# Sums of squares of X's third chunk added by TensorE, and the scores of two query blocks in one visit to the 64x32 tiling

## The chip, the core and the metric

One NeuronCore of a Trainium2 chip runs the whole program; there is one launch. The time of a run is the device time of that core in microseconds (us), and smaller is better. TensorE (PE; its weight loads are the row PEld) multiplies matrices into PSUM. VectorE (DVE), ScalarE (ACT) and GpSimd (POOL) work element by element. SyncE (SP) issues the DMA transfers.

## What is computed

A two-layer decoder trunk runs for 1024 prompt tokens and 32 sample tokens (8 sequences of 4), 1056 columns of width 1024. Both layers begin with an RMSNorm. Layer 0 projects to a causal convolution branch and to a dilated sliding-window attention with 16 heads of 64; layer 1 is a gated linear recurrence. The change touches the first norm and the attention scores of the prompt:

```python
def rms_norm(x, g):
    y = xf * lax.rsqrt(jnp.mean(xf * xf, axis=-1, keepdims=True) + NORM_EPS)

def dswa_prompt(q, k, v, window, dilation):      # (128,1), (512,4), (2048,16), merged
    scores = jnp.einsum('ndbqhe,ndbkhe->ndbhqk', qb, kk) * (hd ** -0.5)
    scores = jnp.where(mask, scores, -jnp.inf)
    p = jnp.exp(scores - lse[..., None])
```

## The kernel before

**Layout.** Everything is held with features on the 128 partitions and tokens along the free dimension. The tokens are cut into three chunks of 384, 384 and 288 columns (`CW`). A dense projection of 128 output features is 24 products for each chunk: eight slices of the contraction, each split into a high and a low part of the reduced float32 format, three products a slice. The projections of layer 0 run pair of heads by pair of heads in the order ag, av (convolution branch), v, k, q.

**The first norm.** x isn't normalised before the projection; the factor `R` (one over the root mean square of a token) is multiplied in where a result leaves PSUM. `prologue()` loads x as twelve tiles `X[c, k]`, chunk c, k from 0 to 3; each holds two feature slices side by side, so 768 or 576 columns. ACT squares each tile. DVE adds them: tile 0 takes tile 1, tile 2 takes tile 3, tile 0 takes tile 2 (`add`), and then tile 0's two halves are added (`fold`). `stat(c)` sums over the partitions on TensorE with a full float32 product against a constant matrix (`self.ones`); such a product shows in the trace as two passes, written x<-b,c. ACT then makes `R` of it by a logarithm and an exponential (`rstd_of`), and POOL multiplies the rotary tables by it (`turn`).

**The attention.** `attention(pr)` handles a pair of heads in 8 blocks of 128 queries. `qk(i)` makes the scores of block i: for each of four groups of 32 queries and two heads a product with a 64-row contraction and 32 output rows, so TensorE works in its 64x32 tiling with eight tiles. The near keys are the 128 (block 0) or 256 keys that end with the block, read one after the other. For blocks from 2 on a second set follows in the same visit, the far keys, 32*i of them and read with a step of 4. Each product has two passes, so a set is 16 passes. The two heads' scores go to two PSUM banks (kind x, four in all). DVE then adds the mask and takes the row minimum (one custom instruction per head), and ACT takes the exponential. `tr(i)` transposes the probabilities, `far(i)` those of the far keys, `pv(i)` multiplies by the values into the bank o, and `far_pv` adds the far part.

**Who sets the order.** The order on every engine is fixed when the program is built. `dense()` emits the projections; after every slice `sides()` puts in atoms, the small pieces of the threads (statistics, attention, convolution, recurrence), by a planner that keeps a clock for each engine (`self.clk`) from prices written in `array()` and `cost()`. A TensorE atom goes in when its due time is at least 300 ns behind TensorE's clock, a bank of kind x is free within 60 ns, and neither ACT's nor DVE's planned clock is over 1500 ns ahead:

```python
if a.kind == "pe":
    ok = r <= now + LEAD and self.xrel[0] <= now + 60 and max(c["act"], c["dve"]) <= now + 1500
```

The price of an addition on DVE is `n / 0.96 + 150` ns for n columns. A result of the first projection (ag, pair 0) leaves PSUM, in the planner's order, after the statistics of all three chunks. Every instruction is issued through the helper at line 158, so that the profile shows L158 throughout; tiles are told apart by their letters (d, x, o are PSUM banks, b and c buffers in SBUF).

Of the kernel before, what the change touches and what calls it, by code (L numbers as in the profile page):

```python
# [11 lines left out]
AF = mybir.ActivationFunctionType  # L12
OP = mybir.AluOpType
# [16 lines left out]
NMASK = 7 * 32 + 256  # L30
# [147 lines left out]
class Kern:  # L178
# [306 lines left out]
    def plan(self, jobs):  # L485
        for j in jobs:
            if j.w is None:
                j.w = W = {"raw": None, "hl": None, "src": j.src}
                self.wq.append(W)

    def w_load(self, W):
        if W["raw"] is None and W["hl"] is None:
            self.own(self.wown, lambda: W.update(raw=self.A.alloc(1024)))
            self.begin(self.clk["pe"])
            self.nc.sync.dma_start(W["raw"].f, W["src"])
            W["t"] = self.cur
# [163 lines left out]
    def prologue(self):  # L660
        nc, A, io = self.nc, self.A, self.io
# [4 lines left out]
        X = {}  # L666
# [7 lines left out]
        def do(f, key, *deps):  # L674
            self.begin(max(at[d] for d in deps))
            f()
            at[key] = self.finish()
# [25 lines left out]
        def square(c, k, act):  # L703
            x = X[c, k]
            if act:
                f = lambda: nc.scalar.activation(x.f, x.f, AF.Square)
            else:
                f = lambda: nc.gpsimd.tensor_tensor(x.f, x.f, x.f, op=OP.mult)
            do(f, ("s", c, k), ("l", c, k))

        def add(c, k, m, eng):
            x, y = X[c, k], X[c, m]
            do(lambda: eng.tensor_tensor(x.f, x.f, y.f, op=OP.add), ("s", c, k), ("s", c, k), ("s", c, m))
            y.free()

        def fold(c):
            w = CW[c]
            x = X[c, 0]
            do(lambda: nc.vector.tensor_tensor(x[:, :w], x[:, :w], x[:, w:2 * w], op=OP.add), ("s", c, 0), ("s", c, 0))

        def stat(c):
            def f():
                w = CW[c]
                x = X[c, 0]
                p = self.px()
                nc.tensor.matmul(p[:, :w], self.ones.f, x[:, :w], start=True, stop=True)
                self.rstd_of(self.R[:, C0[c]:C0[c] + w], p[:, :w])
                x.free()
            return f

        def turn(c):
            def f():
                cs = slice(C0[c], C0[c] + CW[c])
                for t in (self.cos, self.sin):
                    nc.gpsimd.tensor_tensor(t[:, cs], t[:, cs], self.R[:, cs], op=OP.mult)
            return f

        n = KT // 2
        at = {}
# [33 lines left out]
        V = nc.vector  # L773
        for c in range(3):
            for k in range(n):
                square(c, k, True)
            add(c, 0, 1, V)
            add(c, 2, 3, V)
            add(c, 0, 2, V)
            fold(c)  # L780
        for c in range(3):
            self.fin["pro", c] = at["s", c, 0]
            self.spawn(f"pro{c}", 0.1 * c, [Atom(stat(c), "pe", [("pro", c)], ("r0", c)),
                                            Atom(turn(c), "pool", None, ("cs", c))])

# [169 lines left out]
    def attention(self, pr):  # L955
        nc, A = self.nc, self.A
        S = self.pair[pr]
        P, O, B, F = {}, {}, {}, {}

        def width(i):  # L960
            return 32 * i * (i > 1), 128 * min(i + 1, 2)

        def qk(i):
            def f():
                if i == 0:
                    S["den"] = A.alloc(16)
                    S["o"] = A.alloc(T)
                nf, nn = width(i)
                W = nf + nn
                kc = slice(128 * (i + 1) - nn, 128 * (i + 1))  # L970
                hs = [slice(64 * h, 64 * h + 64) for h in range(2)]
                ss = []
                for h in range(2):
                    P[i, h] = A.alloc(W + 8)
                    ss.append(self.px())
                q, k = S["q"], S["k"]
                for a, b, ks in ((nf, W, kc), (0, nf, None)):
                    for r in range(4):
                        for h in range(2):
                            if b > a:  # L980
                                nc.tensor.matmul(ss[h][32 * r:32 * r + 32, a:b],
                                                 q[hs[h], 128 * i + 32 * r:128 * i + 32 * r + 32],
                                                 k[hs[h], ks or slice(r, 128 * i, 4)], start=True, stop=True,
                                                 skip_group_check=True, tile_position=(64 * h, 32 * r))
                t = self.cur
                for h in range(2):
                    e = P[i, h]
                    m = e[:, W:W + 1]
                    self.resume(t)
                    nc.vector.tensor_tensor_reduce(e[:, :W], ss[h][:, :W], self.mask[:, NMASK - W:NMASK],  # L990
                                                   op0=OP.add, op1=OP.min, scale=-0.125, scalar=1e30, accum_out=m)
                    nc.scalar.activation(e[:, :W], e[:, :W], AF.Exp, scale=-1.0, bias=m,
                                         accum_out=S["den"][:, h * 8 + i:h * 8 + i + 1])
            return f

        def tr(i):
            def f():
                nf, nn = width(i)
                p = self.px()
                m = nn // 128  # L1000
                for j in range(m):
                    for h in range(2):
                        n = 2 * j + h
                        nc.tensor.transpose(p[:, 128 * n:128 * n + 128], P[i, h][:, nf + 128 * j:nf + 128 * j + 128],
                                            self.ident)
                B[i] = A.alloc(512)
                self.copy(B[i][:, :256 * m], p[:, :256 * m])
                if not nf:
                    for h in range(2):
                        P[i, h].free()  # L1010
            return f

        def far(i):
            def f():
                p = self.px()
                parts = [n for n, (t0, t1, g, m) in enumerate(FAR) if t0 <= i < t1]
                for n, x in enumerate(parts):
                    g, m = FAR[x][2:]
                    for h in range(2):
                        a = 256 * n + 128 * h  # L1020
                        nc.tensor.transpose(p[:, a:a + 128], P[i, h][:, 128 * g:128 * g + 128], self.ident)
                for h in range(2):
                    P[i, h].free()
                t = self.cur
                for n, x in enumerate(parts):
                    t0, t1, g, m = FAR[x]
                    if i == t0:
                        F[x] = A.alloc(256 * (t1 - t0))
                    self.resume(t, "pe")
                    self.copy(F[x][0:m, :].rearrange("p (h t c) -> p h t c", h=2, c=128)[:, :, i - t0, :],  # L1030
                              p[0:m, 256 * n:256 * n + 256].rearrange("p (h c) -> p h c", h=2))
            return f
# [41 lines left out]
        atoms = [Atom(store, "sp", [("rk", pr, c) for c in range(3)] + [("rq", pr, c) for c in range(3)], ("ko", pr))]  # L1074
        K = lambda n, i: (n, pr, i)
        for i in range(9):
            if i < 8:
                atoms.append(Atom(qk(i), "pe", [K("pv", i - 2)] if i > 1 else [("ko", pr)], K("qk", i),
                                  (2, 7) if i == 0 else None))
            if i:  # L1080
                t = i - 1
                atoms.append(Atom(tr(t), "pe", [K("qk", t)], K("tr", t)))
                if t > 1:
                    atoms.append(Atom(far(t), "pe", [K("qk", t)], K("far", t)))
                atoms.append(Atom(pv(t), "pe", [K("tr", t), ("vt", pr)] + [K("fp", 0)] * (t == 4), K("pv", t)))
                if t % 4 == 3:
                    atoms.append(Atom(far_pv(t // 4), "pe", [K("pv", t)] + [K("far", x) for x in range(max(2, t - 3), t + 1)],
                                      K("fp", t // 4)))
# [1547 lines left out]
```

## Time and profile before

| | before |
|---|---|
| median of 3 runs | 2325.9 us (2324.64 to 2326.06) |
| the profiled execution | 2328.87 us, its span 2327.0 us |
| TensorE busy | 2262.7 us (97%), 17415 passes |
| VectorE busy | 1601.6 us (69%) |
| ScalarE busy | 1026.3 us (44%) |
| GpSimd busy | 1026.5 us (44%) |
| mean granted TensorE clock | 0.994 |

The profile is of one execution, 3.0 us above the median. A matmul's end is modelled, so the starts of following instructions are the firmer numbers. Idle time stands in brackets ahead of an instruction, with what ended it.

### The profile page before, as it was taken

How to read it: one execution, taken by the hardware profiler on the slowest of the kernel's cores; microseconds unless marked ns; L12 is line 12 of the kernel's file. 1: busy time of each engine (PE TensorE's matmuls, PEld its weight loads, DVE VectorE, ACT ScalarE, POOL GpSimd, SP SyncE). 2: the span in 40 equal slices, each digit the busy share in tenths (PEclk: the TensorE clock that was granted, in tenths of full speed). 3: DMA queues.
4: the chain of work that ended last, by engine and by line, in shares of the span. 5: the costliest groups of instructions: out<-in, count | busy, mean ns of one | idle time of the engine just before them, and what ended most of it. 6: DMA issues, size and time to landing. Idle time of an engine off the chain costs nothing.

```text
span 2327.0 us, 42803 instructions
## 1 busy us (share of the span) xinstructions
PE 2262.7 (97%) x17415; PEld 2116.6 (91%) x17415; DVE 1601.6 (69%) x2477; ACT 1026.3 (44%) x1862; POOL 1026.5 (44%) x678
## 2 busy tenths in 40 slices
PE   7999999999999999999999999999999999999997
PEld 7988888888887788899989999999999999998997
DVE  7999899898996557533865666666766666667436
ACT  5454444444444322332564444444454444454422
POOL 4554474645555423543633333333333333344435
PEclk9999999999999999999999999999999999999999
DMA  5121231221247977962541111111121111132426
GB/s 172 49 86 32 76 87 41 78 76 49 70 155 266 342 282 271 331 225 78 187 149 65 65 65 65 65 65 65 47 85 65 65 65 65 65 123 72 168 88 200
DMA packets 118173, 271.60 MB, mean 117 GB/s; under 512 B 32336, under 2 KB 59472, under 8 KB 117968
## 3 DMA queue, kind: packets, MB, share of 16 engines
q1 hardware_dynamic: 117968, 268.78, 33.9%
q8 instruction: 139, 2.28, 0.4%
q14 instruction: 66, 0.54, 0.1%
HBM read 215.00 MB, written 53.73 MB: 115 GB/s over the span
## 4 chain that ended last, share of the span: by engine, by line
PE 68%; DVE 14%; issue 7%; DMA 4%; POOL 3%; ACT 3%; SPq 0%; POOLq 0%; DVEq 0%; ACTq 0%
PE d L158 38%; PE x L158 29%; DVE b L158 14%; POOL b L158 3%; ACT b L158 2%; DMA b<-kc 1%; PE o L158 1%; DMA b<-ybd 1%; DVE c L158 1%; DMA b<-wab 1%; SPq L158 0%; DMA b<-rd 0%; DMA b<-vc 0%; POOL c L158 0%; DMA b<-x 0%
## 5 line engine op out<-in xcount | busy, mean ns | idle before, releaser
L158 PE MATMUL d<-c,b 128*128 128x384 f32 (+1 forms) x7920 | 1387.7, 329 | 8.4 <-ACT b L158 7.8
L158 PEld LDWEIGHTS d<-c,b 128*128 128x128 f32 x7920 | 1279.3, 189 | 53.8 <-issue 40.3
L158 POOL TENSOR_TENSOR b<-b,b 128x1024 fp32r<-128x1024 f32 (+5 forms) x401 | 827.3, 2076 | 835.0 <-ACT b L158 637.3
L158 ACT ACTIVATE b<-b 128x384 f32<-128x384 f32 (+15 forms) x647 | 358.2, 569 | 804.7 <-DVE b L158 786.4
L158 PE MATMUL x<-c,b 128*128 128x384 f32 (+3 forms) x3616 | 583.8, 312 | 11.8 <-ACT b L158 5.3
L158 PEld LDWEIGHTS x<-c,b 128*128 128x128 f32 (+1 forms) x3616 | 540.1, 175 | 30.1 <-ACT b L158 8.8
L158 DVE TENSOR_TENSOR b<-b,b 128x384 f32<-128x384 f32 (+13 forms) x296 | 316.9, 1081 | 89.1 <-ACT b L158 71.4
L158 DVE SCALAR_TENSOR_TENSOR b<-b,c,b 128x1024 f32<-128x1024 f32 (+1 forms) x218 | 364.3, 1671 | 9.9 <-ACT b L158 7.5
L158 PE MATMUL x<-b,b 128*32 128x128 f32 (+12 forms) x4552 | 286.7, 338 | 6.4 <-DVE b L158 5.7
L158 DVE SCALAR_TENSOR_TENSOR b<-b,b 128x384 f32<-128x384 f32 (+3 forms) x216 | 188.3, 877 | 105.7 <-ACT b L158 101.4
L158 PEld LDWEIGHTS x<-b,b 64*32 64x32 f32 (+3 forms) x4552 | 205.6, 128 | 57.6 <-issue 37.4
L158 ACT CAST b<-b 128x1024 fp32r<-128x1024 f32 (+3 forms) x264 | 224.6, 861 | 18.8 <-DMA b<-woc 5.2
L158 DVE TENSOR_TENSOR b<-d,b 128x384 f32<-128x384 f32 (+3 forms) x278 | 139.8, 509 | 127.8 <-PE d L158 124.3
L158 DVE TENSOR_TENSOR b<-x,b 128x288 f32<-128x288 f32 (+3 forms) x164 | 83.3, 508 | 136.2 <-PE x L158 121.7
L158 POOL TENSOR_SCALAR b<-b 128x32 f32<-128x32 f32 x40 | 27.3, 682 | 295.2 <-DVE b L158 269.6
L158 ACT COPY b<-x 128x512 f32<-128x512 f32 (+4 forms) x175 | 85.4, 496 | 159.1 <-PE x L158 143.4
L158 DVE COPY b<-x 128x512 f32<-128x512 f32 (+7 forms) x219 | 102.5, 479 | 73.6 <-PE x L158 66.6
L158 ACT COPY b<-d 32x384 f32<-32x384 f32 (+2 forms) x212 | 94.8, 447 | 114.7 <-DVE b L158 77.9
L158 ACT ACTIVATE b<-b,c 128x512 f32<-128x512 f32 (+2 forms) x114 | 96.3, 869 | 3.6 <-DVE b L158 1.2
L158 DVE CUSTOM_DVE_ANT_0 b<-x,b 128x128 f32<-128x128 f32 (+8 forms) x144 | 72.0, 533 | 34.4 <-PE x L158 32.7
L158 POOL COPY b<-b 128x32 f32<-128x32 f32 (+1 forms) x105 | 59.1, 573 | 69.0 <-DVE b L158 67.3
L158 DVE TENSOR_TENSOR b<-b,x 128x128 f32<-128x128 f32 x144 | 53.9, 374 | 36.9 <-PE x L158 32.7
(61 smaller groups left out, 968.2 us busy)
## 6 DMA issues: line engine op xcount, KB each, us to landing
b<-wc SPq DMA_DIRECT2D x64, 512.0 KB, 4.2
b<-wab SPq DMA_DIRECT2D x56, 512.0 KB, 5.8
b<-kc SPq DMA_DIRECT2D x64, 448.0 KB, 6.3
b<-vc SPq DMA_DIRECT2D x64, 448.0 KB, 8.3
b<-woa SPq DMA_DIRECT2D x32, 512.0 KB, 3.7
b<-woc SPq DMA_DIRECT2D x32, 512.0 KB, 4.2
b<-yd SPq DMA_DIRECT2D x16, 528.0 KB, 6.2
ybd<-b SPq DMA_DIRECT2D x16, 512.0 KB, 3.0
```

The costliest lines, as they stand in the source:

```text
L158: r = f(*a, **k)
```

## The change

In the prologue the last two additions of the third chunk (c = 2) on DVE are left out. `stat(2)` makes four products instead of one: the two halves of tile 0 and the two halves of tile 2, accumulated in one bank; tile 2 is freed there. In the attention `qk` takes one or more blocks. Blocks 0 and 1 of a pair are made by one atom: 16 passes of 128 columns and 16 of 256 columns in one visit, into the same two banks side by side (384 columns), followed by the four reductions and exponentials, block by block. Each block still reports its own finish to the planner.

```diff
         def stat(c):
             def f():
                 w = CW[c]
-                x = X[c, 0]
                 p = self.px()
-                nc.tensor.matmul(p[:, :w], self.ones.f, x[:, :w], start=True, stop=True)
+                xs = [X[c, k] for k in ((0, 2) if c == 2 else (0,))]
+                parts = [x[:, a:a + w] for x in xs for a in ((0, w) if c == 2 else (0,))]
+                for n, x in enumerate(parts):
+                    nc.tensor.matmul(p[:, :w], self.ones.f, x, start=(n == 0), stop=(n == len(parts) - 1))
                 self.rstd_of(self.R[:, C0[c]:C0[c] + w], p[:, :w])
-                x.free()
+                for x in xs:
+                    x.free()
...
             add(c, 0, 1, V)
             add(c, 2, 3, V)
-            add(c, 0, 2, V)
-            fold(c)
+            if c < 2:
+                add(c, 0, 2, V)
+                fold(c)
         for c in range(3):
-            self.fin["pro", c] = at["s", c, 0]
+            self.fin["pro", c] = max(at["s", c, 0], at["s", c, 2] if c == 2 else 0)
...
-        def qk(i):
+        def qk(*blocks):
+
             def f():
-                if i == 0:
+                if blocks[0] == 0:
...
+                ss = [self.px() for h in range(2)]
+                off, at = {}, 0
+                for i in blocks:
+                    off[i] = at
+                    at += sum(width(i))
+                for i in blocks:
...
                 t = self.cur
-                for h in range(2):
-                    e = P[i, h]
-                    m = e[:, W:W + 1]
-                    self.resume(t)
-                    nc.vector.tensor_tensor_reduce(e[:, :W], ss[h][:, :W], self.mask[:, NMASK - W:NMASK],
...
+                for i in blocks:
+                    W = sum(width(i))
+                    for h in range(2):
+                        e = P[i, h] = A.alloc(W + 8)
+                        m = e[:, W:W + 1]
+                        self.resume(t)
+                        nc.vector.tensor_tensor_reduce(e[:, :W], ss[h][:, off[i]:off[i] + W],
...
+                    self.fin["qk", pr, i] = max(self.end, self.cur)
...
         for i in range(9):
-            if i < 8:
-                atoms.append(Atom(qk(i), "pe", [K("pv", i - 2)] if i > 1 else [("ko", pr)], K("qk", i),
-                                  (2, 7) if i == 0 else None))
+            if i < 8 and i != 1:
+                atoms.append(Atom(qk(*((i,) if i else (0, 1))), "pe", [K("pv", i - 2)] if i else [("ko", pr)], None,
+                                  None if i else (2, 7)))
```

## Rows read from the trace of the kernel before

**Rows 1.** The page, busy time of each engine and its share of the span.
```profile
PE 2262.7 (97%) x17415; PEld 2116.6 (91%) x17415; DVE 1601.6 (69%) x2477; ACT 1026.3 (44%) x1862; POOL 1026.5 (44%) x678
```

**Rows 2.** TensorE's timeline, 28 to 42 us: start, duration, instructions, idle time before.
```profile
28.95 1.45 PE L158 MATMUL x<-b,c 128*128 128x384 f32 x4
29.95 1.49 PE L158 MATMUL x<-c,b 128*128 128x384 f32 x6
35.76 1.30 PE L158 MATMUL x<-b,c 128*128 128x288 f32 x2 [4.32 <-DVE b L158]
```

**Rows 3.** VectorE's timeline, 28 to 41 us, additions of chunk 2 one by one.
```profile
28.59 2.93 DVE L158 TENSOR_TENSOR b<-b,b 128x576 f32<-128x576 f32 x1
31.44 1.55 DVE L158 TENSOR_TENSOR b<-b,b 128x576 f32<-128x576 f32 x1
33.02 1.43 DVE L158 TENSOR_TENSOR b<-b,b 128x576 f32<-128x576 f32 x1
34.48 1.13 DVE L158 TENSOR_TENSOR b<-b 128x288 f32<-128x288 f32 x1
```

**Rows 4.** Stretches: PE, PEld, DVE, ACT, POOL busy us, then granted clock, DMA share, GB/s.
```profile
31.50:34.60 3.10, 0.00 (x0) 0.00 (x0) 3.03 (x4) 0.46 (x1) 3.10 (x3) 1.00 0.00 0
34.70:41.40 6.70, 5.64 (x19) 5.39 (x20) 2.41 (x4) 3.15 (x5) 3.33 (x4) 0.50 0.00 1
```

**Rows 5.** Groups by shape, 1203.1 to 1205.8 us: count, busy us, mean ns of one.
```profile
L158 PE MATMUL x<-b,c 128*128 128x288 f32 x5 | 1.4, 406 | 0.0
```

**Rows 6.** TensorE's timeline about 1203 and 28 us, single runs at the full clock.
```profile
1202.81 1.38 PE L158 MATMUL x<-b,c 128*128 128x288 f32 x5
27.74 1.37 PE L158 MATMUL x<-c,b 128*128 128x384 f32 x7
```

**Rows 7.** TensorE's timeline, two later waits.
```profile
780.21 0.77 PE L158 MATMUL x<-c,b 128*128 128x128 f32 x5 [1.65 <-ACT b L158]
2130.35 1.18 PE L158 MATMUL x<-b,b 128*128 128x128 f32 x4 [1.87 <-DVE b L158]
```

**Rows 8.** Busy time by stretch behind those two waits.
```profile
778.50:783.00 4.50, 2.49 (x10) 0.75 (x9) 0.96 (x3) 4.37 (x9) 0.00 (x0) 1.00 0.99 378
2130.50:2137.20 6.70, 5.17 (x19) 4.87 (x20) 5.32 (x9) 1.26 (x3) 2.34 (x1) 0.50 0.11 24
```

**Rows 9.** TensorE's timeline, 93 to 96 us: blocks 0 and 1, first pair.
```profile
93.64 0.34 PE L158 MATMUL d<-c,b 128*128 128x384 f32 x1
93.91 0.45 PE L158 MATMUL x<-b,b 64*32 64x128 f32 x16
94.29 0.79 PE L158 MATMUL d<-c,b 128*128 128x384 f32 x3
95.01 0.66 PE L158 MATMUL x<-b,b 64*32 64x256 f32 x16
95.60 0.62 PE L158 MATMUL d<-c,b 128*128 128x384 f32 x2
```

**Rows 10.** TensorE's timeline, visits of blocks 2 and 4 of the same pair.
```profile
101.30 0.89 PE L158 MATMUL x<-b,b 64*32 64x256 f32 x32
102.12 0.44 PE L158 MATMUL d<-c,b 128*128 128x384 f32 x1
116.09 1.14 PE L158 MATMUL x<-b,b 64*32 64x256 f32 x32
117.16 0.44 PE L158 MATMUL d<-c,b 128*128 128x384 f32 x1
```

**Rows 11.** Groups by shape in block 0's visit, then in block 4's.
```profile
L158 PE MATMUL x<-b,b 64*32 64x128 f32 x16 | 0.4, 281 | 0.0
L158 PE MATMUL x<-b,b 64*32 64x128 f32 x16 | 0.7, 397 | 0.0
```

**Rows 12.** Waits of TensorE, 94 to 740 us: us in total, times, longest.
```profile
PE o L158 <- DVE b L158: 9.4, 13, 1.6
```

**Rows 13.** VectorE's timeline, 94 to 98 us, between the reductions of blocks 0 and 1.
```profile
94.88 3.50 DVE L158 SCALAR_TENSOR_TENSOR b<-b,c,b 128x1024 f32<-128x1024 f32 x1
```

More of the change, by code (lines that the diff above doesn't have):

```diff
@@ L961, in width @@
             return 32 * i * (i > 1), 128 * min(i + 1, 2)
-        def qk(i):
+        def qk(*blocks):
             def f():
-                if i == 0:
+                if blocks[0] == 0:
                     S["den"] = A.alloc(16)
                     S["o"] = A.alloc(T)
-                nf, nn = width(i)
-                W = nf + nn
-                kc = slice(128 * (i + 1) - nn, 128 * (i + 1))
                 hs = [slice(64 * h, 64 * h + 64) for h in range(2)]
-                ss = []
-                for h in range(2):
-                    P[i, h] = A.alloc(W + 8)
-                    ss.append(self.px())
@@ L976, in f @@
                 q, k = S["q"], S["k"]
[L977 to L984, printed above, removed]
@@ L985, in f @@
-                t = self.cur
-                for h in range(2):
-                    e = P[i, h]
-                    m = e[:, W:W + 1]
-                    self.resume(t)
-                    nc.vector.tensor_tensor_reduce(e[:, :W], ss[h][:, :W], self.mask[:, NMASK - W:NMASK],
-                                                   op0=OP.add, op1=OP.min, scale=-0.125, scalar=1e30, accum_out=m)
-                    nc.scalar.activation(e[:, :W], e[:, :W], AF.Exp, scale=-1.0, bias=m,
-                                         accum_out=S["den"][:, h * 8 + i:h * 8 + i + 1])
+                ss = [self.px() for h in range(2)]
@@ new lines, in f @@
+                off, at = {}, 0
[3 more added lines that the diff above has]
+                for i in blocks:
+                    nf, nn = width(i)
+                    W = nf + nn
+                    kc = slice(128 * (i + 1) - nn, 128 * (i + 1))
+                    for a, b, ks in ((nf, W, kc), (0, nf, None)):
+                        for r in range(4):
+                            for h in range(2):
+                                if b > a:
+                                    nc.tensor.matmul(ss[h][32 * r:32 * r + 32, off[i] + a:off[i] + b],
+                                                     q[hs[h], 128 * i + 32 * r:128 * i + 32 * r + 32],
+                                                     k[hs[h], ks or slice(r, 128 * i, 4)], start=True, stop=True,
+                                                     skip_group_check=True, tile_position=(64 * h, 32 * r))
@@ new lines, in f @@
+                t = self.cur
+                for i in blocks:
+                    W = sum(width(i))
+                    for h in range(2):
+                        e = P[i, h] = A.alloc(W + 8)
+                        m = e[:, W:W + 1]
+                        self.resume(t)
+                        nc.vector.tensor_tensor_reduce(e[:, :W], ss[h][:, off[i]:off[i] + W],
+                                                       self.mask[:, NMASK - W:NMASK],
+                                                       op0=OP.add, op1=OP.min, scale=-0.125, scalar=1e30, accum_out=m)
+                        nc.scalar.activation(e[:, :W], e[:, :W], AF.Exp, scale=-1.0, bias=m,
+                                             accum_out=S["den"][:, h * 8 + i:h * 8 + i + 1])
+                    self.fin["qk", pr, i] = max(self.end, self.cur)
```

## The prediction

> **What bounds the kernel now.** The page comes first: TensorE is busy for 97% of the span, VectorE for 69% [rows 1]. So what an edit is worth is read on TensorE: either it takes passes away, or it shortens a wait. Its timeline at the start of the run shows the one long wait inside the kernel. TensorE makes the statistics of chunks 0 and 1 at 28.95 us, six dense products from 29.95, and stands still for 4.32 us until the statistic of chunk 2 begins at 35.76 [rows 2]. What releases it is VectorE: the timeline of that engine shows the four additions of chunk 2 one behind the other, ending at 31.52, 32.99, 34.45 and 35.61 [rows 3]. The last of them ends 0.15 us before the statistic. The stretches show a second price of this wait. The granted clock is still 1.00 (2.4 GHz) up to 34.6 and then 0.50 (1.2 GHz) from 34.7 to at least 41.4, while TensorE is back at work from 35.76 [rows 4]. Waits like this one are where a few microseconds lie; the second edit works on something else, the way into and out of another tiling of the array, which is in TensorE's timeline around 94 us [rows 9].
>
> **First edit, the statistic of chunk 2.** It removes VectorE's third and fourth additions (33.02 and 34.48). The first two products read tile 0, complete at 31.52; the last two read tile 2, complete at 32.99. I keep these two times, since the edit changes nothing ahead of them on VectorE. It adds three products. Each is two passes of 288 columns; five such passes one behind the other take 1.38 us, of which the last lasts 0.41 [rows 5, 6], so a pass takes (1.38 - 0.41)/4 = 0.24 us at the full clock.
>
> Now the new course, with the same 0.15 us from VectorE to TensorE. Four passes can run from 31.67 to 32.64, in time that was idle. The third product starts at 32.99 + 0.15 = 33.14, and four passes are still to do. Before, two passes were to do at 35.76. So the start comes 35.76 - 33.14 = 2.62 us earlier, and two passes, 0.48 us, are added behind it. That is 2.1 us.
>
> The clock is on top. Before, TensorE worked from 35.76 to 41.4 at half speed and so lost half of 5.6 us, 2.8 us. In the new course its longest idle stretch here is under 1.6 us (below). In this trace a wait of 1.65 us left the clock at 1.00 over its stretch, and one of 1.87 us was followed by 0.50 [rows 7, 8]. So I expect no fall of the clock and 2.8 us back. Sum so far: 2.1 + 2.8 = 4.9 us.
>
> Against that stands the planner. It lets statistics in only when VectorE's planned clock is at most 1.5 us ahead, and by its own price the two removed additions are 576/0.96 + 150 = 750 and 288/0.96 + 150 = 450 ns. All three statistics should therefore come about 1.2 us earlier in TensorE's order. Seven dense products take (1.37 us for a run of seven) about 1.2 us [rows 6]; these stood ahead of the wait and covered part of it, and will stand behind it. TensorE would then reach the third statistic at about 30.2 and idle for some 1.4 us, then 0.5 us. This costs 1.2 us: 4.9 - 1.2 = 3.7 us, which I take. The upper end is 4.9 (order kept). The lower end is a clock that falls all the same: at 1.0 for the 1.5 us from 33.14 to 34.64, then at half; of 0.97 (four passes) + 2.3 (dense products that before were done by 41.4 at half speed, 2.8 less the two passes) + 1.2 = 4.5 us of work, 3.0 us would be left at 34.64 and take 6.0 us, to 40.6. That is 0.8 us gained.
>
> Who waits behind the third statistic: on TensorE the dense products of av (0.5 us, counted); on ScalarE the logarithm and exponential of chunk 2, which come earlier with it; on VectorE the first result of the projection, which stood behind the fourth addition and now moves up by 2.6 us. No DMA moves.
>
> **Second edit, blocks 0 and 1 in one visit.** It removes no pass. It removes one change of tiling per pair, and there are eight pairs. Block 0: the dense product ahead starts at 93.64, the first pass at 93.91, so 0.27 us instead of the 0.17 us that a dense product takes in a run of its kind [rows 6, 9]: 0.10 us for the way in. From the first pass to the next dense product are 0.38 us for 128 columns and, in block 1, 95.60 - 95.01 = 0.59 us for 256 [rows 9]. The two visits cost 0.48 + 0.69 = 1.17 us.
>
> No visit of 128 and 256 contiguous columns is in the trace. The nearest are those that follow 256 contiguous columns with a strided set: 0.82 us with 64 columns, 1.07 with 128 [rows 10]. 64 more strided columns cost 0.25 us, so with none it would be 0.57, which is the 0.59 of block 1: a second set costs its columns and nothing fixed. Its columns are dear only as they are strided: a pass of 128 lasts 397 ns in block 4 and 281 ns in block 0 [rows 11]. Contiguous, 128 more columns cost 0.59 - 0.38 = 0.21 us. The merged visit then is 0.10 + 0.59 + 0.21 = 0.90 us and saves 0.27; by 128 columns at the strided price it is 0.10 + 1.07 = 1.17 and saves nothing. The first row is nearer, since block 1's keys are contiguous; I take 0.25 us, 2.0 us for eight pairs, between 0 and 3.0 (a 128-column set wholly hidden but for its way out, 0.38 us a pair).
>
> Here the page "TensorE: Matmul & The Clock Gate" of the Trainium skill speaks against the edit: in its part on packing small matmuls it says that a weight load runs beside products in flight only where the row group differs. The second block's loads go to the same row groups as the first block's products. By that rule they would wait and the saving would shrink to nothing, 2.0 us less in the sum. The rows of the second sets, which load weights into the same groups, show no such fixed price.
>
> VectorE does the same four reductions per pair, but block 0's now waits for up to 32 passes instead of 16, some 0.2 us, and the two banks stay taken until four reductions are through. In return block 1's reduction no longer has to stand behind a convolution step, which in the first pair held it for 3.50 us [rows 13].
>
> **Sum.** 3.7 + 2.0 = 5.7 us. The profiled execution lasted 2328.87 us with 2327.0 of span, 3.0 above the median; I take the difference from the median: 2325.9 - 5.7 = 2320.2 us. With both edits at their ends it is 2318.0 to 2325.1.
>
> **Rivals.**
> First, the clock falls all the same, as two idle stretches (1.4 and 0.5 us) lie close together: 0.8 + 2.0 = 2.8 us, 2323.1. For it speaks that 1.65 and 1.87 us are a thin line; against it that eight passes stand between.
> Second, VectorE sets the pace from 94 to 740 us. TensorE waits there 9.4 us for it at the bank o alone, 13 times [rows 12]. VectorE's work is unchanged there, and it starts earlier only by what the statistic's end is earlier: that end was at about 37.06 (35.76 + 1.30) and will be at about 34.3, so 2.8 us. The second edit's gain would be eaten by longer waits: 2323.1. Against it: these waits are short and scattered, with long busy runs of TensorE between.
> Third, a second set costs its loads after all, and 3.7 us alone remain: 2322.2. This is where the page's rule would lead; the rows of the second sets speak against it.
> Fourth, slower: the first transposition of every pair comes to wait for VectorE, since block 0's reduction starts later and a convolution step (3.50 us, rows 13) gets ahead of the other three. The price of such a wait is up to 1.6 us, the longest at the bank o [rows 12]; it turns the sign from 0.71 us a pair (5.7/8) and at 1.6 us makes 12.8 - 5.7 = 7.1 us, 2333.0. It needs the planner to leave a hole there on VectorE in most pairs.
> Under all cases lies a spread: the planner lays the whole order anew, and its many short waits of TensorE are dealt again. Of 9.4 us in 13 waits I allow 2.5 us either way.
>
> **How the numbers follow.** Forecast 0.56, clock 0.12, VectorE 0.16, loads 0.06, slower 0.10. The range 2315.5 to 2326.5 takes the lower end with the spread below it and the three middle cases with theirs, and leaves out most of the slower case. What a measurement can tell from no change is about 0.2%, 4.65 us, so faster begins below 2321.25. The forecast lies 1.0 us under that line, and with the spread some seven tenths of it count as faster, 0.39, and of the three middle cases three in ten, 0.10: 0.49. Slower by 4.65 us is most of the fourth case, 0.08. The rest, 0.43, is within.
>
> **What would show it.** TensorE's timeline: eight passes of 288 columns in two groups, the second beginning near 33.1, no wait over 1.7 us, the clock at 1.00 from 34 to 42. VectorE: two additions of 576 columns instead of three, none of 288. Visits: 56 of 64x32 instead of 64, the merged one some 0.8 us from first pass to the next dense product. The waits at the bank o between 94 and 740 us stay near 9.4 us in total. The prediction is wrong if the clock still falls near 34 us, if the merged visit takes 1.07 us or more, or if those waits grow by over 3 us.

## The result and the profile after

| | before | after |
|---|---|---|
| median | 2325.9 us (2324.64 to 2328.17) | 2314.96 us (2314.93 to 2317.08) |
| the profiled execution | 2328.87 us, span 2327.0 | 2314.96 us, span 2313.1 |
| TensorE's idle time from 94 to 740 us | 15.6 us | 6.6 us |

The ratio of the times is 0.9949, interval 0.9939 to 0.9960: 10.9 us less, where 5.7 were forecast, and 0.5 us below the range. The profiled execution of before lies 3.0 us above its median, so the two traces differ by more than the medians, 13.9 us of span.

The page's busy times after; TensorE and VectorE answer to [rows 1]:

```profile
PE 2261.0 (98%) x17421; PEld 2119.5 (92%) x17421; DVE 1593.4 (69%) x2459; ACT 1029.6 (45%) x1876; POOL 1042.4 (45%) x680
```

TensorE's timeline of after around the statistics (start, duration, then the instructions in a run, their number, and in brackets the idle time ahead and who ended it); it answers to [rows 2]:

```profile
29.08 0.91 PE L158 MATMUL x<-b,c 128*128 128x384 f32 x2 [0.19 <-DVE b L158]
29.54 0.97 PE L158 MATMUL x<-c,b 128*128 128x384 f32 x3
32.01 1.21 PE L158 MATMUL x<-b,c 128*128 128x288 f32 x4 [1.50 <-DVE b L158]
33.39 1.24 PE L158 MATMUL x<-b,c 128*128 128x288 f32 x4 [0.17 <-DVE b L158]
34.25 2.46 PE L158 MATMUL x<-c,b 128*128 128x384 f32 x12
```

The wait of 4.32 us is gone; 1.50 and 0.17 us stand in its place, with the eight passes in two groups. Three dense products lie between the second and the third statistic where six lay before. VectorE's timeline of after, against [rows 3], shows two additions of 576 columns, none of 288, and the first result of the projection behind them at 33.26 instead of 35.53:

```profile
28.94 4.39 DVE L158 TENSOR_TENSOR b<-b,b 128x576 f32<-128x576 f32 x2
33.26 0.55 DVE L158 TENSOR_TENSOR b<-d,b 128x384 f32<-128x384 f32 x1
```

The stretches of after (start and end, length, busy time of PE, PEld, DVE, ACT and POOL with instructions, then the granted clock, DMA share and GB/s); the first two answer to [rows 4]:

```profile
31.50:34.60 3.10, 2.42 (x9) 1.68 (x10) 2.30 (x3) 0.00 (x0) 3.10 (x3) 1.00 0.00 0
34.70:41.40 6.70, 6.70 (x46) 6.70 (x45) 2.91 (x8) 4.57 (x8) 2.97 (x4) 1.00 0.00 0
94.00:740.00 646.00, 639.41 (x6016) 555.98 (x6014) 582.73 (x799) 301.58 (x674) 374.66 (x224) 1.00 0.29 89
```

The clock stays at 1.00 where it was at 0.50. The third row is the stretch of the attention. TensorE's idle time in it is 646.00 - 639.41 = 6.6 us. The same view of the kernel before gives 646.00 - 630.43 = 15.6:

```profile
94.00:740.00 646.00, 630.43 (x5934) 542.27 (x5938) 580.70 (x808) 297.32 (x659) 349.91 (x218) 1.00 0.28 87
```

Who ended TensorE's waits there after the change (total, times, longest); the first row answers to [rows 12], 9.4 us:

```profile
PE o L158 <- DVE b L158: 4.2, 13, 0.8
PE x L158 <- DVE b L158: 1.2, 5, 0.4
PE x L158 <- ACT b L158: 0.6, 2, 0.4
```

The merged visit of the first pair, in TensorE's timeline of after and by form (total busy time, mean ns); it answers to [rows 9, 11]:

```profile
91.52 0.51 PE L158 MATMUL d<-c,b 128*128 128x384 f32 x2
91.96 0.88 PE L158 MATMUL x<-b,b 64*32 64x128 f32 x32
92.78 0.96 PE L158 MATMUL d<-c,b 128*128 128x384 f32 x4
```
```profile
L158 PE MATMUL x<-b,b 64*32 64x256 f32 x16 | 0.6, 376 | 0.0
L158 PE MATMUL x<-b,b 64*32 64x128 f32 x16 | 0.5, 281 | 0.0
```

From the first pass to the next dense product are 92.78 - 91.96 = 0.82 us, for 128 and 256 columns together.

**Where the 13.9 us of the traces lie.** The same dense product, the 161st, starts at 45.96 us before and at 43.02 after, while the 72nd, ahead of the statistics, starts at 22.58 and 22.75: the prologue gives 3.1 us. The visits give eight times 0.26, 2.1 us. The waits from 94 to 740 us give 9.0. The two edits account for about 5; the largest part is waits that no edit names.

### The profile page after: what moved, and what is told of

The parts are those of the page before. It is cut to its first block, busy times and chain, and to the rows that moved or that the text cites. A ratio compares the mean times of both kernels' runs of the same rounds, so it can differ in the third digit from the quotient of the medians.

```text
span 2313.1 us, 42853 instructions
## 1 busy us (share of the span) xinstructions
PE 2261.0 (98%) x17421; PEld 2119.5 (92%) x17421; DVE 1593.4 (69%) x2459; ACT 1029.6 (45%) x1876; POOL 1042.4 (45%) x680
## 4 chain that ended last, share of the span: by engine, by line
PE 58%; DVE 5%; issue 4%; DMA 3%; POOL 2%; ACT 1%; SPq 0%; POOLq 0%; ACTq 0%; DVEq 0%
PE d L158 31%; PE x L158 27%; DVE b L158 5%; POOL b L158 2%; DMA b<-kc 1%; ACT b L158 1%; DMA b<-vc 1%; DMA b<-ybd 0%; PE o L158 0%; DMA b<-wab 0%; DMA yad<-b 0%; DMA b<-yd 0%; SPq L158 0%; DMA b<-x 0%; DVE c L158 0%
## 5 line engine op out<-in xcount | busy, mean ns | idle before, releaser
L158 POOL TENSOR_TENSOR b<-b,b 128x512 f32<-128x512 f32 (+6 forms) x403 | 836.7, 2088 | 827.0 <-ACT b L158 620.3
L158 PE MATMUL x<-c,b 128*128 128x384 f32 (+4 forms) x3592 | 577.8, 311 | 6.5 <-ACT b L158 3.4
L158 PEld LDWEIGHTS x<-c,b 128*128 128x128 f32 (+2 forms) x3592 | 535.4, 175 | 21.7 <-ACT b L158 5.6
L158 DVE TENSOR_TENSOR b<-b,b 128x384 f32<-128x384 f32 (+14 forms) x293 | 318.4, 1096 | 83.4 <-ACT b L158 67.0
L158 DVE TENSOR_TENSOR b<-x,b 128x384 f32<-128x384 f32 (+3 forms) x163 | 82.7, 507 | 136.7 <-PE x L158 122.2
L158 ACT COPY b<-x 128x512 f32<-128x512 f32 (+5 forms) x189 | 89.7, 489 | 138.5 <-PE x L158 130.2
L158 DVE COPY b<-x 128x512 f32<-128x512 f32 (+8 forms) x205 | 96.1, 480 | 71.2 <-PE x L158 66.1
```

The lines of the kernel that those rows point to most:

```text
L158: r = f(*a, **k)
```

## The experiments

Three theories stood at the start; the expectations weigh them. **D, the dealt order**: the planner lays the whole order anew after any change, and the waits from 94 to 740 us are a property of the order dealt, whatever instruction it was dealt for. **V** (P in some expectations): VectorE sets the pace there, and the waits are shorter since its work begins earlier. **M**: with four reductions one behind the other, the merged visit itself shortens the waits. Idle time below is TensorE's from 94 to 740 us in the profiled run, as above; that is one execution of each kernel. Times are medians, with the kernel before timed beside each group, and the interval of the difference is taken from that of the ratio.

### Each edit alone, and a nudge of the planner

stat_only is the change without its edits in `attention`, merge_only the change without those in `prologue`; both let the planner lay the order. The other two change one price of the planner's and no instruction: before_over in the kernel before, after_over in the changed one.

```diff
-OVER = dict(dve=83.0, act=95.0, pool=54.0)
+OVER = dict(dve=80.0, act=95.0, pool=54.0)
```

> The first edit alone: third chunk's last additions go to TensorE, the attention as before. The changed kernel gained 10.9 us by the medians; in its profile 2.9 us stand at the dense products behind the statistics, about 2.1 us are the eight merged visits, and the rest is in fewer waits of TensorE between 94 and 740 us (15.6 us of idle time before, 6.6 after). Theory M (the merged reductions shorten those waits): this kernel gains about 3 us and keeps about 15 us of idle time there. Theory V (the head start of VectorE shortens them): it gains 8 to 9 us. Theory D (the order is dealt anew and the waits fall by chance): anything from 0 to 8 us, with the idle time there unlike both profiles.

> The second edit alone: the prologue as before, blocks 0 and 1 in one visit. Theory M: it gains 2 us for the visits and 5 to 6 us in waits, about 2318, with some 7 us of idle time between 94 and 740 us. Theory V: 2 us, 2324. Theory D: 2 us plus or minus what another order gives, and the waits need not be near those of the changed kernel. In every case the prologue keeps the wait of 4.3 us and the clock of 0.50 behind it.

> The kernel before with one number of the planner changed and no instruction added or removed: the planned overlap of VectorE's instructions is 80 ns instead of 83, so that the order differs from about 50 us on. It measures what another order alone does. Theory D: the time moves by 2 to 6 us either way, and the idle time of TensorE between 94 and 740 us moves with it. Theories M and V: within 2 us of the kernel before, idle time there near 15 us.

> The changed kernel with the same one number of the planner changed (80 ns instead of 83). Theory D: it loses some of the 10.9 us, up to 6 us of it, by longer waits between 94 and 740 us. Theories M and V: within 2 us of the changed kernel, idle time there near 7 us.

| | this / before | ratio, interval | difference, us | idle, us |
|---|---|---|---|---|
| stat_only | 2327.73 / 2327.04 | 1.0003 [0.9993, 1.0013] | +0.7 [-1.6, +3.0] | 18.8 |
| merge_only | 2319.81 / 2327.04 | 0.9965 [0.9953, 0.9976] | -7.2 [-10.9, -5.6] | 9.1 |
| before_over | 2341.58 / 2327.04 | 1.0057 [1.0040, 1.0074] | +14.5 [+9.3, +17.2] | 18.5 |
| after_over | 2327.13 / 2327.04 | 0.9996 [0.9984, 1.0008] | +0.1 [-3.7, +1.9] | 17.9 |

A price 3 ns lower, with the work the same, costs the kernel before 14.5 us and takes from the changed one its whole gain. stat_only's prologue is 3.0 us shorter in the trace and its time is not. So the order is a term as large as the edits.

The planner deals more than the order. By its clocks it also chooses which engine makes a copy out of PSUM, and so with some sums and differences:

```python
    def copy(self, o, i):
        if self.clk["act"] <= self.clk["dve"]:
            self.nc.scalar.copy(o, i)
        else:
            self.nc.vector.tensor_copy(o, i)
```

The page of after shows it against [rows 1]: VectorE has 18 instructions fewer, of which the edit removes two; ScalarE has 14 more and GpSimd two. "Order" stands for both below.

In before_over it works in three places, shown by its stretches:

```profile
200.00:300.00 100.00, 93.70 (x903) 79.73 (x887) 86.27 (x123) 45.56 (x102) 51.81 (x34) 0.98 0.24 67
...
740.00:1100.00 360.00, 345.18 (x3091) 305.81 (x3076) 198.70 (x351) 125.17 (x219) 154.94 (x123) 1.00 0.73 266
```

and by the same two of before:

```profile
200.00:300.00 100.00, 97.15 (x927) 83.11 (x933) 93.24 (x124) 46.45 (x102) 57.83 (x36) 1.00 0.25 69
...
740.00:1100.00 360.00, 352.72 (x3055) 318.96 (x3048) 191.34 (x346) 123.88 (x212) 155.42 (x120) 1.00 0.70 256
```

Idle time grows from 2.9 to 6.3 us in the first stretch and from 7.3 to 14.8 in the second, and the first has a clock of 0.98, 2 us of its 100 lost. The idle time from 94 to 740 us is thus not all that an order changes. The clock is another part: its mean over the executions is 0.9922 in before_over and 0.9946 in the 22 of before beside them. Where TensorE sets the pace, 0.0024 of 2327 us is some 5.6 us of the 14.5, an estimate. It also makes much of the scatter of one kernel: after_over took 2318.79 us at 0.997 and 2329.89 at 0.992.

### The edits in the order of the kernel before

Here the planner still prices the old work, and so deals the old order; only the instructions named are others. A switch does it, `mode2`: "priced" is reckoned and not emitted, "unpriced" is emitted and not reckoned.

```diff
-            self.kern.fill(self.eng)
-            r = f(*a, **k)
-            self.kern.account(self.eng, name, a, k)
+            if self.kern.mode2 != "unpriced":
+                self.kern.fill(self.eng)
+            r = f(*a, **k) if self.kern.mode2 != "priced" else None
+            if self.kern.mode2 != "unpriced":
+                self.kern.account(self.eng, name, a, k)
```

stat_fixed is the first edit. merge_fixed moves block 1's 16 passes next to block 0's and leaves its reductions where they were. merge_red_fixed moves these too, behind block 0's. both_fixed is stat_fixed with merge_fixed.

```diff
             add(c, 2, 3, V)
+            self.mode2 = "priced" if c == 2 else None
             add(c, 0, 2, V)
             fold(c)
+            self.mode2 = None
...
+                self.mode2 = "priced" if i == 1 else None
+                products(i, ss, ((nf, W, kc), (0, nf, None)))
+                self.mode2 = None
+                if i == 0:
+                    self.mode2 = "unpriced"
+                    products(1, [x[:, 128:384] for x in ss], ((0, 256, slice(0, 256)),))
+                    self.mode2 = None
```

> The first edit alone, with the order of every engine kept as in the kernel before: the planner still reckons with the two additions on VectorE and with one product, while the program has four products and no such additions. Theory D (what the first edit lost when run alone went into the order dealt anew): 4 to 5 us faster than before, with some 4.9 us at the dense products behind the statistics (no product moved behind the wait) and most of it left at the end. Theory P (VectorE sets the pace from 94 to 740 us and takes back whatever TensorE gains): about 5 us behind the statistics, but under 2.5 us at the end, and longer waits of TensorE in between.

> The merged visit alone, order kept: the 16 passes of block 1 go in with block 0's, and nothing else moves on any engine; the reductions of block 1 stay where they were, behind a convolution step. The planner reckons as before. Theory D: 2 us faster (eight visits at 0.26 us), with waits between 94 and 740 us like those before, 15 us of idle time give or take 2. Theory M (merging shortens the waits): only with the reductions moved up, so here also 2 us. Theory P: less than 1 us.

> As the run before, and block 1's two reductions and exponentials directly behind block 0's, ahead of the convolution step that stood between them; in each pair this one step moves, and nothing else. Theory M: 5 to 8 us faster than the kernel before, idle time between 94 and 740 us down to about 9 us. Theory D: as without the move, within 1.5 us.

> Both edits with the order of the kernel before kept (reductions of block 1 in their old places). Theory D: the sum of the two parts, 6 to 7 us faster, and less than the changed kernel's 10.9 us, because the rest of that came from its own order. Theory M: 7 us. Theory P: 2 to 3 us.

| | this / before | ratio, interval | difference, us | idle, us |
|---|---|---|---|---|
| stat_fixed | 2325.54 / 2326.64 | 0.9993 [0.9983, 1.0003] | -1.1 [-4.0, +0.7] | 15.9 |
| merge_fixed | 2330.65 / 2326.64 | 1.0010 [1.0000, 1.0020] | +4.0 [0.0, +4.7] | 19.3 |
| merge_red_fixed | 2331.12 / 2326.64 | 1.0013 [1.0003, 1.0023] | +4.5 [+0.7, +5.4] | 18.6 |
| both_fixed | 2325.31 / 2326.64 | 0.9992 [0.9982, 1.0001] | -1.3 [-4.2, +0.2] | 18.5 |

In the old order neither edit, nor both, makes the kernel faster by an amount that this timing can tell from nothing. M falls in this order: with the reductions together the kernel is slower. merge_fixed loses by idle time, 3.7 us more, and by the clock, with a mean of 0.9939 against 0.9948, an estimated 2 us, against the 2.1 that the visits save. And the waits stay with the order. The wait of the third pair at the bank o is found again in each of these kernels, whatever was changed ahead of it: before, stat_fixed and merge_fixed show it in TensorE's timelines as

```profile
273.64 0.66 PE L158 MATMUL o<-b,b 128*64 128x128 f32 x8 [1.60 <-DVE b L158]
```
```profile
269.05 0.55 PE L159 MATMUL o<-b,b 128*64 128x128 f32 x6 [1.46 <-DVE b L159]
```
```profile
275.94 0.55 PE L159 MATMUL o<-b,b 128*64 128x128 f32 x6 [1.59 <-DVE b L159]
```

and both_fixed and merge_red_fixed at 271.12 and 272.81 with 1.61 each. stat_fixed reaches it 4.6 us sooner and waits about as long, so VectorE came that much sooner too: V's bound is not there.

What the merged visit loses in this order is seen in the second pair. TensorE's timeline of before, and then of merge_fixed:

```profile
185.64 0.44 PE L158 MATMUL o<-b,b 128*64 128x128 f32 x4
```
```profile
187.08 0.44 PE L159 MATMUL o<-b,b 128*64 128x128 f32 x4 [1.10 <-DVE b L159]
```

VectorE's timeline ahead of it, of before, and one line of GpSimd's:

```profile
181.44 0.29 DVE L158 CUSTOM_DVE_ANT_0 b<-x,b 128x128 f32<-128x128 f32 x1
...
181.87 1.28 DVE L158 SCALAR_TENSOR_TENSOR b<-b,c,b 128x1024 f32<-128x1024 f32 x1
...
183.75 0.42 DVE L158 COPY b<-x 128x256 f32<-128x256 f32 x1
```
```profile
181.97 3.45 POOL L158 TENSOR_TENSOR b<-b,b 128x1024 fp32r<-128x1024 f32 x1 [1.61 <-ACT b L158]
```

and the same of merge_fixed:

```profile
182.28 0.29 DVE L159 CUSTOM_DVE_ANT_0 b<-x,b 128x128 f32<-128x128 f32 x1 [0.34 <-PE x L159]
...
182.71 3.28 DVE L159 SCALAR_TENSOR_TENSOR b<-b,c,b 128x1024 f32<-128x1024 f32 x1
...
186.61 0.41 DVE L159 COPY b<-x 128x256 f32<-128x256 f32 x1
```
```profile
182.52 2.39 POOL L159 TENSOR_TENSOR b<-b,b 128x1024 fp32r<-128x1024 f32 x1 [1.63 <-ACT b L159]
```

Block 0's reduction waits 0.34 us for the longer visit. Before, the convolution step behind it began 0.10 us ahead of GpSimd's product; it took 1.28 us, and GpSimd's 3.45. Now it begins 0.19 us behind, takes 3.28 us, and GpSimd's 2.39. The copy that the products at the bank o read ends at 187.02 instead of 184.17, 2.85 us later where the reduction began 0.84 later, and TensorE waits 1.10 us for it. By these rows the engine that started first went through and the other was held. The rest of before's trace fits. It has 186 of these convolution steps from 94 to 740 us. The 53 with no GpSimd instruction beside them lasted 1.18 to 1.29 us. The 90 that began while a GpSimd instruction ran ended, every one, 1.08 to 1.10 us after that instruction's end, and lasted up to 3.47. Of the 43 that began ahead of GpSimd's, 42 lasted 1.23 to 1.29; the one of [rows 13], ahead by 0.02 us, was held all the same. The Trainium skill's page "SBUF — State Buffer", section "SBUF: two separate sides", says that a GpSimd operation that reads SBUF and a VectorE operation with two inputs from SBUF exclude each other for a whole instruction, and that the first to start goes through; the trace agrees, but for that one case at 0.02 us.

### The order of the changed kernel with the old statistic

unstat_order takes the changed kernel's order and merged visits, and makes the statistic of chunk 2 as before: all four additions on VectorE and one product.

```diff
+                self.mode2 = "priced" if c == 2 else None
                 for n, x in enumerate(parts):
...
+                if c == 2:
+                    self.mode2 = "unpriced"
+                    nc.tensor.matmul(p[:, :w], self.ones.f, X[2, 0][:, :w], start=True, stop=True)
...
+                V.tensor_tensor(X[2, 0].f, X[2, 0].f, X[2, 2].f, op=OP.add)
+                V.tensor_tensor(X[2, 0][:, :CW[2]], X[2, 0][:, :CW[2]], X[2, 0][:, CW[2]:2 * CW[2]], op=OP.add)
```

> The order of the changed kernel on every engine, but the statistic of the third chunk made as before: both additions back on VectorE, one product on TensorE; the planner reckons as in the changed kernel. Theory D (the order dealt anew holds the rest of the gain): 5 us of the statistic are lost and all else stays, so 5 to 6 us faster than the kernel before, with 6 to 8 us of idle time between 94 and 740 us. Theory V (the head start of VectorE shortens the waits): the idle time there goes back to 12 us or more and the time to within 3 us of the kernel before.

It took 2320.45 us against 2328.76, a ratio of 0.9966 [0.9954, 0.9977], so -8.3 us [-10.7, -5.4]. Its wait for the statistic, a stretch behind it and its waits at the bank o from 94 to 740 us, from the timeline, the stretches and the waits:

```profile
35.93 1.30 PE L159 MATMUL x<-b,c 128*128 128x288 f32 x2 [5.61 <-DVE b L159]
```
```profile
34.00:39.40 5.40, 3.47 (x10) 3.22 (x11) 2.21 (x3) 2.08 (x3) 3.72 (x5) 0.50 0.01 2
...
94.00:740.00 646.00, 639.43 (x6036) 555.19 (x6035) 582.58 (x807) 303.35 (x677) 376.37 (x226) 1.00 0.29 88
```
```profile
PE o L159 <- DVE b L159: 4.2, 13, 0.8
```

The wait of 5.61 us and the half clock are back, and the waits from 94 to 740 us are after's: 6.6 us in all, 4.2 at the bank o. V falls. In its trace the 161st dense product starts 3.7 us later than after's: that is what the first edit is worth in this order by the traces. By the times it is 2.6 us (8.3 against 10.9). The rest of the gain comes with the order and the merged visits. What the order would do with separate visits was not run.

### Other orders, with separate and with merged visits

Does an order that is planned around merged visits wait less (M')? Prices of the planner's were changed in kernels with separate visits (the kernel before, stat_only) and with merged ones (the changed kernel, merge_only), one number each: `LAT` of VectorE 33 to 30 (_lat30), of ScalarE 33 to 36 (_act), `OVER` of VectorE 83 to 80 (_over), `QUEUE` 800 to 820 (_q820) or 780 (_queue).

```diff
-LAT = dict(pe=54.0, dve=33.0, act=33.0, pool=78.0)
+LAT = dict(pe=54.0, dve=30.0, act=33.0, pool=78.0)
...
-QUEUE = 800
+QUEUE = 820
```

> The kernel before with another number of the planner changed (VectorE's planned latency 30 ns instead of 33), no instruction added or removed; the order differs from about 30 us on. One more deal of the unmerged kernel. Theory D: time within 15 us either way, idle time between 94 and 740 us anywhere from 6 to 20 us. Theory M' (an order planned around merged visits has shorter waits as a rule): 15 to 19 us of idle time there, as in the three unmerged orders so far (15.6, 18.5, 18.8).

> The kernel before with the planner's queue limit 820 ns instead of 800: another order with separate visits. Theory M': 14 to 19 us of idle time of TensorE between 94 and 740 us. Theory D: 6 to 20.

> First edit alone, planned overlap of VectorE 80 ns instead of 83: one more order with blocks 0 and 1 in separate visits. Theory M' (an order planned around merged visits waits less): 14 to 19 us of idle time of TensorE between 94 and 740 us, as in the unmerged orders so far (14.7, 15.6, 18.5, 18.8). Theory D (chance): anything from 6 to 20.

> First edit alone, ScalarE's planned latency 36 ns instead of 33: another order with separate visits. Theory M': 14 to 19 us of idle time between 94 and 740 us. Theory D: 6 to 20.

> Second edit alone, planned overlap of VectorE 80 ns instead of 83; its order differs from the second edit's own from about 200 us on. Another order with merged visits. Theory M': below 12 us of idle time between 94 and 740 us. Theory D: 6 to 20.

> Second edit alone, VectorE's planned latency 30 ns instead of 33: another order with merged visits. The merged orders so far had 6.6, 7.6, 9.1, 17.8 and 17.9 us of idle time between 94 and 740 us. Theory M': below 12 us. Theory D: 6 to 20.

> Second edit alone, the planner's queue limit 820 ns instead of 800: another order with merged visits. Theory M': below 12 us of idle time between 94 and 740 us. Theory D: 6 to 20.

> The changed kernel with one number of the planner changed (its queue limit 780 ns instead of 800), no instruction added or removed; the order differs from about 50 us on. One more deal of the merged kernel. Theory D: idle time between 94 and 740 us anywhere from 6 to 20 us, and the time up to 12 us above the changed kernel. Theory M': 6 to 10 us of idle time there, as in two of the three merged orders so far (6.6, 9.1, 17.9).

> The changed kernel with ScalarE's planned latency 36 ns instead of 33, no instruction added or removed. One more deal of the merged kernel; expectations as for the run before: theory D 6 to 20 us of idle time between 94 and 740 us, theory M' 6 to 10 us.

| | this / before | ratio, interval | difference, us | idle, us |
|---|---|---|---|---|
| separate: before_lat30 | 2330.87 / 2328.76 | 1.0013 [1.0003, 1.0022] | +2.1 [+0.7, +5.1] | 14.7 |
| before_q820 | 2334.17 / 2328.02 | 1.0022 [1.0011, 1.0034] | +6.2 [+2.6, +7.9] | 16.8 |
| stat_only_over | 2320.08 / 2326.97 | 0.9969 [0.9958, 0.9981] | -6.9 [-9.8, -4.4] | 16.2 |
| stat_only_act | 2328.49 / 2326.97 | 1.0004 [0.9993, 1.0015] | +1.5 [-1.6, +3.5] | 15.7 |
| merged: merge_only_over | 2329.37 / 2328.02 | 1.0011 [0.9994, 1.0028] | +1.3 [-1.4, +6.5] | 19.0 |
| merge_only_lat30 | 2327.54 / 2326.97 | 1.0002 [0.9991, 1.0013] | +0.6 [-2.1, +3.0] | 12.6 |
| merge_only_q820 | 2319.24 / 2326.97 | 0.9973 [0.9953, 0.9992] | -7.7 [-10.9, -1.9] | 9.2 |
| after_queue | 2324.88 / 2328.76 | 0.9983 [0.9974, 0.9993] | -3.9 [-6.1, -1.6] | 16.7 |
| after_act | 2319.14 / 2328.76 | 0.9962 [0.9948, 0.9977] | -9.6 [-12.1, -5.4] | 7.6 |

With before, after and the first four, there are seven orders for separate visits, with 14.7 to 18.8 us of idle time, and eight for merged ones: 6.6, 7.6, 9.1, 9.2, 12.6, 16.7, 17.9 and 19.0 (the 16.7 is after_queue's, which an expectation above lists as 17.8). Five of the eight lie below all seven, three do not. As a rule M' falls; whether merging makes short waits likelier is open. One thing does go with them: how many of the copies out of the banks x from 94 to 740 us ScalarE was given. It made 81 to 83 of them in the five orders with the least idle time, 78 in after_queue, and 65 to 72 in all others, the seven with separate visits included. No run moved copies alone, so who makes them stands as an untested rival to chance. Every order with under 10 us is faster by 7 us or more, but stat_only_over is so with 16.2. The order that the change was dealt has the least idle time of all fifteen, and no version is told from it as faster.

## Why the prediction was wrong

**The statistic: right in the traces, a little large.** The two groups, the shorter waits (1.50 and 0.17 us for 1.4 and 0.5), the start of the third product (33.39 for 33.14, in an execution whose first pass starts at 8.18 us instead of 7.82) and the clock at 1.00 came as worked out. From the 72nd dense product to the 161st the prologue gained 3.1 us in after, 3.0 in stat_only, 3.8 in stat_only_over, and 3.9 between unstat_order and after, for 3.7 forecast; with the order kept 4.6, for the 4.9 of the upper end. So the planner's part was there too, 1.5 us (4.6 less 3.1) for 1.2.

**The visit: right.** 0.82 us stand for the 0.80 forecast, and the visit saves 0.26 us for 0.25. A second set costs its columns and no fixed price, and the third rival falls. In after's trace eight weight loads run from 92.21 to 92.36 us while a pass is in flight on each of the eight tiles (begun at 92.21 to 92.25, 0.38 us each). The Trainium skill's page "TensorE: Matmul & The Clock Gate" says in its part on packing that a load overlaps with products in flight only where the row group differs; these loads and the 0.82 us contradict that. The same part also names a load into the background weight buffer as one that is pulled ahead, which fits. A pass of the 128 columns takes the 281 ns of block 0 [rows 11], also with another set behind it, and not the 397 of the strided one; the 256 columns behind take 376.

**The failed step is the spread.** "Of 9.4 us in 13 waits I allow 2.5 us either way", and that these waits "stay near 9.4 us in total". They became 4.2 at the bank o, and TensorE's idle time in the stretch fell by 9.0 us. Over the orders tried, the same work differs by 14.5 us in the kernel before (four orders), by 8.4 in stat_only (three), by 9.0 in merge_only (four) and by 11.0 in the changed kernel (four). I saw that the order is laid anew, and held its effect for a scatter of 2.5 us under the forecast, while it was the largest term. That the deal went the right way was luck: in after_over the same work takes as long as the kernel before. In the order of before the edits' own sum isn't reached either: -1.3 us [-4.2, +0.2] for both, in part as the merged visits bring new waits there (18.5 us idle for 15.6).

**The rivals.** The second, that VectorE sets the pace, fell twice (stat_fixed's wait stays, unstat_order's waits don't return). The fourth is real as a mechanism: in merge_fixed's second pair a convolution step is held and TensorE comes to wait 1.10 us for VectorE, though at the bank o and not at the first transposition. Whether after's order avoids this elsewhere was not traced. My 3.50 us for that step [rows 13] was not its price but that of starting beside GpSimd's product, which began at 94.90 us and took 2.39: alone the step lasts 1.28. The first, the falling clock, did not occur in after and did in one other kernel with the first edit, below.

**Open.** stat_fixed's trace is 4.9 us ahead of before's at the 161st dense product and still 4.7 at the 2993rd, at 701 us, and that execution was the fastest of its ten, 2321.61 us; its median gains only 1.1. The clock on record tells a part: its mean is 0.9952 over the ten and 0.9948 over before's 31, some 0.9 us, where 2.8 were forecast. What takes the rest in the other executions no trace here shows. Nor is it settled by what an order comes to wait less. One such reason, the turn between VectorE and GpSimd, was seen in merge_fixed's second pair; its amount isn't what differs, since the convolution steps from 94 to 740 us lose 80 us to it in before and 82 in after. The share of ScalarE in the copies goes with the waits and wasn't tested by itself.

## What to carry to other kernels

Where a planner or a scheduler lays the order anew, change one of its prices by a few per cent (here 2.5 to 9), several times, before and after an edit: the spread of these times is the error of any forecast made from the edit alone, and here it was 8 to 15 us against edits of 2 to 4 us. To measure an edit by itself, keep the order and change only the instructions. And the best of several dealt orders may be worth more than the edit that it was dealt for.

## What the runs showed of the hardware that was not expected

The same idle time at TensorE lowered the clock in one kernel and not in others. stat_only and stat_only_act have the same passes and waits at the third statistic; TensorE's timelines of stat_only, then of stat_only_act, and the granted clock from 33.2 us of each (columns as for the stretches above):

```profile
31.29 1.21 PE L158 MATMUL x<-b,c 128*128 128x288 f32 x4 [1.50 <-DVE b L158]
32.66 1.24 PE L158 MATMUL x<-b,c 128*128 128x288 f32 x4 [0.17 <-DVE b L158]
```
```profile
31.39 1.21 PE L158 MATMUL x<-b,c 128*128 128x288 f32 x4 [1.49 <-DVE b L158]
32.77 1.98 PE L158 MATMUL x<-b,c 128*128 128x288 f32 x4 [0.17 <-DVE b L158]
```
```profile
33.20:36.40 3.20, 3.20 (x19) 3.04 (x19) 0.00 (x0) 2.40 (x4) 3.20 (x5) 1.00 0.00 0
```
```profile
33.20:36.40 3.20, 3.20 (x10) 2.77 (x9) 0.00 (x0) 1.56 (x3) 2.84 (x4) 0.50 0.00 0
```

With 1.50 us of waiting the clock stays at its 2.4 GHz, and with 1.49 it falls to 1.2 GHz; the prologue's gain there is 1.4 us instead of 3.0. The profiled executions of after, after_over, after_queue and after_act have the same two waits (1.50, 1.50, 1.49 and 1.51 us, then 0.17) and kept it. In [rows 7, 8] a wait of 1.65 us left the clock and one of 1.87 was followed by the lower one. So the length of the wait alone doesn't decide here, and after's gain of the clock need not come in every execution.
